# Normalising the input rows on ScalarE, moving four memory products between the first head products, and making the lower parts of the memory weights on VectorE

## The chip, the cores and the metric

The kernel runs on one core of one Trainium2 chip. The metric is device microseconds (us) of one execution, as the median of several runs; lower is better. In the profile PE is TensorE (products), PEld its weight loads, DVE is VectorE, ACT is ScalarE, POOL is GpSimd and SP is the engine that issues most DMAs.

## The reference

One inference step of a decoder layer (model width 1024) for 1024 prompt tokens and 8 decode tokens. Cut to what matters here:

```python
xp = layer_norm(x_prompt, ln_in_g, ln_in_b)          # 1024 rows of 1024
xs = layer_norm(x_sample, ln_in_g, ln_in_b)          # 8 rows
mk, mv = (mem @ w_kv)                                # 256 memory rows, w_kv 1024 x 2048: keys, values
proj = x @ w_in + b_in                               # q, k, v, o of 4 heads, 8 gates, pool input, x-attention q, branch gates
y_m = mLSTM(q, k, v, gates) ; y_p = pool_mix(u) ; y_x = attention(xq, mk, mv)
x = layer_norm(ALPHA * x + (g0*y_m + g1*y_p + g2*y_x) @ w_o)
x = layer_norm(ALPHA * x + conv_gated_ffn(x))
```

`layer_norm` takes a row's mean and variance, subtracts and divides, then applies a gain and an offset per feature. The memory's keys and values do not depend on x; they are needed by the outputs and by the attention, long after the mLSTM heads have begun.

## The kernel before, in words

**Units.** All large products are *units*: 128 output columns of some weight, times all token columns, in chunks of 384, 384 and 264 columns (CHUNKS, line 27). Each fp32 weight is split in two parts of 12 bits: an upper part `whi` (ScalarE, line 180) and a lower part `wlo` (line 181), and each k-tile takes three products (upper x upper, upper x x-lower, lower x upper), line 250. `s.pool` chooses the engine of the lower part: GpSimd or VectorE. A split is made in two pieces of 128x512. A memory unit (`kv_unit`, line 456) has one chunk of 256 columns, so 24 products; a head unit has 72; the gate unit has 48.

**The order.** `run_units` (line 183) writes all instructions out in one order, and every engine executes its own in that order. While it writes a unit's products it counts a planning clock, `max(n, 256) / 2400` us for each product of n columns, and after each 0.6 us or more of it calls `tick` (a piece of a weight split, up to NW = 3 weights ahead of the units done; then loads as far as buffers reach, 4 ahead for the memory weights, line 199) and then `side.advance`. Side work lies in two lanes of generators; each yields the planning time until its next step. Lane 0 is stepped before lane 1.

**The opening.** Units 0 to 15 are the memory units. `first` and `second` (lines 493, 499) load the first x tiles, later ones are loaded ahead of units 4 to 9 (line 507), the small rows at unit 10 (`load_rest`), and at unit 14 the gate weights are prepared on VectorE. The x rows lie in nine tiles of 128 tokens (tile 8: the 8 decode rows). Two generators run beside the units:

- `g_rows_in` (line 394, lane 0 from unit 1): step i takes the statistics of tile i on VectorE (`ln_stats`; the power -1/2 on GpSimd, line 366) and normalises tile i-1 in place on VectorE (`normalise`, line 370); then it yields 2.8.
- `g_ln_in` (line 409, lane 1 from unit 3): for each chunk of three tiles it waits until they are normalised, yields 2.0, and then `to_features` (line 377) for each of 8 feature blocks transposes on TensorE, applies gain and offset on ScalarE (`tmp`, line 384), rounds to `xhi` and subtracts to `xlo` on VectorE (lines 386, 387). It yields 1.0 after each block.

Behind the memory units comes the gate unit (line 621). Before each of its chunks it calls `wait_for`, which writes out side steps, without products between, until that chunk of x is there. `tmp` has 3 buffers, the small PSUM tiles 5, the products' PSUM tiles 3. After the gate unit the key and value rows are transposed (`g_kv_rows`, lane 1), and the units of the first head follow in the order k, k, v, v, q, q, o, o (line 783), then three more heads.

**Weights at the start.** The first two memory weights have their lower parts on VectorE, the other 14 on GpSimd (line 490).

Of the kernel before, what the change touches and what calls it, by code (L numbers as in the profile page):

```python
# [14 lines left out]
D = 1024  # L15
# [8 lines left out]
# Token columns, and their token tiles, of products whose rows a layer norm follows.  # L24
PASSES = (((640, 392), (8, 5, 6, 7)), ((256, 384), (2, 3, 4)), ((0, 256), (0, 1)))
# Token columns of one matrix product: three token tiles, three, two and the decode rows.
# [4 lines left out]
# Weights are loaded up to EARLY pieces ahead at the start; each piece is split in PARTS steps, not closer  # L31
# together than SHARE of a unit's length, nor sooner than AGE after its load.
EARLY = 4
PARTS = 2
SHARE = 0.1
AGE = 2.0
# Time, in us, between two looks at the side work.
# [3 lines left out]
class Side:  # L41
    """Work that is put between the large products: lanes of generators, each lane in order. A generator
    yields the time, in us of large products, that passes before its next step."""
# [45 lines left out]
class Split:  # L89
    """Weights, k-tiles of 128 rows and some columns, as two parts of 12 bits each, whose sum is the weight."""  # L90
# [16 lines left out]
def tile_hybrid_step(ctx: ExitStack, tc: tile.TileContext, x_prompt, mem_prompt, x_sample, cache_mem_k,  # L107
# [43 lines left out]
    # The tensor engine's clock rises after some microseconds of work: until the first loads are here.  # L151
# [9 lines left out]
    # ---------------------------------------------------------------- dense products  # L161
# [11 lines left out]
    def split_part(s, k):  # L173
        """One of the PARTS shares of the k-tiles."""
        if k == 0:
            s.hi = weight_tile(s, "whi", NW, F32R)
            s.lo = weight_tile(s, "wlo", NW, F32R)
        n = s.nk // PARTS
        ks = slice(k * n, (k + 1) * n)
        nc.scalar.activation(s.hi[:, ks], s.raw[:, ks], AF.Copy)  # L180
        (nc.gpsimd if s.pool else nc.vector).tensor_sub(s.lo[:, ks], s.raw[:, ks], raw_f(s.hi[:, ks]))  # L181

    def run_units(first_loads):
# [10 lines left out]
        def load_more(first=0):  # L194
            """Loads as far as the buffers reach."""
            while len(here) < len(order):
                n = len(here)
                s = order[n]
                if n < first or n < min(split + 2, free + NW + 1) or s.early and n < split + EARLY:
                    load(s)  # L200
                    here[n] = clock
                else:
                    break

        def tick(us, force=False):
            """Splits, a part at a time, as far as the buffers of the units before reach."""
            nonlocal split, part, clock, last
            clock += us
            if split not in here or not (split < free + NW or order[split].tile):
                return  # L210
            if not force and (clock - last < space or clock - here[split] < AGE):
                return
            last = clock
            split_part(order[split], part)
            part += 1
            if part == PARTS:
                split, part = split + 1, 0
                load_more()
# [55 lines left out]
    def weight_pairs(w2d, c0, ncols, k0=0, nk=8):  # L274
        """[(Split, column)] for each 128 columns of w2d[k0*128:, c0:c0+ncols]."""
        out = []
        wd = min(1024 // nk, ncols)
        for a in range(c0, c0 + ncols, wd):
            s = Split(w2d[k0 * 128:(k0 + nk) * 128, a:a + wd].rearrange("(k p) c -> p k c", p=128), nk, wd)
            out += [(s, c) for c in range(0, wd, 128)]  # L280
        return out
# [6 lines left out]
    # ---------------------------------------------------------------- vectors as columns  # L288
# [59 lines left out]
    # ---------------------------------------------------------------- layer norms  # L348
# [5 lines left out]
    def ln_stats(parts, n):  # L354
        """Mean and 1/deviation of the rows that parts hold side by side."""
        st = sp.tile([128, 2, 6], F32, name=nm("st"), tag="st")
        for i, p in enumerate(parts):
            nc.vector.bn_stats(st[:n, i, :], p)  # L358
        return mean_dev(st, len(parts), n)
# [17 lines left out]
    def to_features(rows, c0, n, g0, b0, wait, per=1):  # L377
        """Transposes normalised rows of one chunk, applies gain and offset, splits into xhi, xlo."""
        for f in range(8):
            p = PS()  # L380
            for j, (t, m) in enumerate(rows):
                nc.tensor.transpose(p[:, j * 128:j * 128 + m], t[:m, f * 128:(f + 1) * 128], ident[:m, :m])  # L382
            tmp = cur[0].tile([128, 392], F32, tag="tmp", bufs=3, name=nm("tmp"))
            nc.scalar.activation(tmp[:, :n], p[:, :n], AF.Identity, bias=colA[:, b0 + f:b0 + f + 1],
                                 scale=colA[:, g0 + f:g0 + f + 1])
            nc.vector.tensor_copy(xhi[:, f, c0:c0 + n], tmp[:, :n])  # L386
            nc.vector.tensor_sub(xlo[:, f, c0:c0 + n], tmp[:, :n], raw_f(xhi[:, f, c0:c0 + n]))  # L387
            if f % per == per - 1:
                yield wait * per
# [4 lines left out]
    def g_rows_in():  # L394
        """x, normalised, by token."""
        st = {}
        for i in range(10):
# [3 lines left out]
            if i:  # L401
                m = rows_of(i - 1)
                normalise(xt[i - 1][:m, :D], xt[i - 1][:m, :D], *st[i - 1], m)
# [3 lines left out]
    def g_ln_in():  # L407
        for c, (c0, n) in enumerate(CHUNKS):
# [3 lines left out]
            yield 2.0  # L412
# [9 lines left out]
    # ================================================================ phase 1: memory keys and values  # L422
# [43 lines left out]
    def g_kv_rows():  # L466
        """Keys and values by memory row, for the outputs and as the second factor of the attention."""
# [19 lines left out]

    for j, (s, c) in enumerate(weight_pairs(w_mem_kv[0], 0, 2048)):
        u = kv_unit(j, s, c)
        s.pool = j > 1  # L490
# [17 lines left out]
        if j == 10:  # L508
            u.before = load_rest
        if j == 14:  # L510
            u.before = lambda: (gate_prepare(), make_conv_cols())
        units.append(u)

    # ================================================================ phase 2: gates of the mLSTM
    # Per token of a tile: a, exp(-m), exp weight of the state, decay; by head. Tile 8: decode rows.
# [10 lines left out]
    class GateSplit:  # L526
        """Both parts of the gates' weights side by side, each multiplied with both parts of x."""
# [20 lines left out]
    def g_gates():  # L548
# [19 lines left out]
        # b: sum of lf within a tile of 128 tokens; mt: running max.  # L568
# [54 lines left out]
    units[-1].after = lambda: side.add(1, "kv_rows", g_kv_rows())  # L623

    # ================================================================ phase 3: mLSTM
# [30 lines left out]
    def halves(hi, lo, src, scale=None):  # L656
        """src, scaled by a column, as two parts of 12 bits each."""
# [7 lines left out]
    def product(out, w, x, first=True, last=True):  # L665
        """out (+)= w^T x, both in two parts."""
# [116 lines left out]
    for h in range(4):  # L783
        for wi, what in enumerate("kvqo"):
            off = {"q": 0, "k": 1024, "v": 2048, "o": 3072}[what] + 256 * h
            for kt, (s, c) in enumerate(weight_pairs(w_in2, off, 256)):
                units.append(head_unit(h, what, kt, s, c))
                if (h, wi, kt) == (0, 0, 0):
                    units[-1].before = lambda: next_phase("phase1")

    def g_sample_mlstm():
        """The decode rows: one step of the recurrence for each of the 32 states."""
# [37 lines left out]
        # For each decode row a block of 40 columns, zero but for the two parts of q: results 0-7 and 32-39.  # L830
# [91 lines left out]
    # ================================================================ phase 4: attention to the memory  # L922
# [91 lines left out]
    # Softmax of the decode rows, by memory row: for each a block of 16 columns with its two parts, else zero.  # L1014
# [109 lines left out]
    def open_gate(b, f):  # L1124
        """The spilled gates come back before their sigmoid."""
# [72 lines left out]
    # ================================================================ phase 5: mLSTM output  # L1198
# [34 lines left out]
    # ================================================================ phase 6: pooling  # L1233
# [5 lines left out]
    def pool_consts():  # L1239
        # sel[15 b + j, g, b'] = (b == b') and j >= 16 - window  # L1240
        nc.gpsimd.memset(sel, 1.0)
        for g in range(4):
            w = 2 << g
            v = sel[:, g, :]
            # 15 b + j - 15 b' - (16 - w) >= 0
            nc.gpsimd.affine_select(out=v, in_=v, pattern=[[-15, 8]], compare_op=OP.is_ge, fill=0.0,
                                    base=-(16 - w), channel_multiplier=1)
            # 15 b' + 14 - (15 b + j) >= 0
# [124 lines left out]
    # ================================================================ phase 7: w_o, first layer norm  # L1373
# [63 lines left out]
    # Each pass goes through the features in the other direction and starts with the weights that are still here.  # L1437
# [14 lines left out]
    # ================================================================ phase 8: gated feed-forward with convolution  # L1452
# [5 lines left out]
    def g_state_conv():  # L1458
        """The two kept rows of each decode row, feature-major: [feature, tile, row, decode row]."""
# [99 lines left out]
    # The first chunk's columns are normalised while the other two chunks are multiplied.  # L1559
# [30 lines left out]
    # ================================================================ phase 9: the last products by chunk, second layer norm  # L1590
# [9 lines left out]
    def ln2_half(t, h):  # L1600
        """Transposes features 512 h.. of a token tile and takes their share of its mean and deviation."""
# [91 lines left out]
```

## Time and profile before

| | |
|---|---|
| median of 3 runs | 2214.84 us (2213.61 to 2218.53) |
| span of the profiled execution | 2210.3 us, 36109 instructions |
| the profiled execution's own time | not listed apart; the three runs lie 3.3 to 8.2 us above the span |
| TensorE busy | 2169.0 us (98%) |
| VectorE, ScalarE, GpSimd busy | 55%, 37%, 16% |
| mean granted TensorE clock | 0.994 of full |

Span and busy times come from one execution under the profiler; the median comes from runs without it. A busy share is a mean over stages with different limits, so it says little of one stage. A wait is named by who waited and by what ended the wait.

### The profile page before, as it was taken

What the parts mean: (1) busy time and instruction counts of PE and PEld (TensorE: products, weight loads), DVE (VectorE), ACT (ScalarE), POOL (GpSimd) and SP (SyncE); (2) the same over time, 40 slices, a digit from 0 to 9 for tenths busy, and PEclk for the clock granted to TensorE, in tenths of its full rate; (3) what the DMA queues carried; (4) which work ended last, traced back from release to release, by engine and by line L of the source; (5) the groups of instructions that cost most, each with busy time, mean ns of one, the idle gap of its engine ahead of it and who ended that gap; (6) DMA issues with size and microseconds to landing.
All of it is one profiled execution on the core that took longest, in us unless ns stands there. A gap on an engine that the chain in (4) does not pass through costs nothing.

```text
span 2210.3 us, 36109 instructions
## 1 busy us (share of the span) xinstructions
PE 2169.0 (98%) x14337; PEld 2140.7 (97%) x14337; DVE 1207.6 (55%) x2776; ACT 826.1 (37%) x1635; POOL 364.5 (16%) x523
## 2 busy tenths in 40 slices
PE   8999999999999999999999999999999999999996
PEld 7899999999999999999999999999999999999996
DVE  6834738383767765635335556644544343443457
ACT  4524343434457543442213333444142341423421
POOL 6301010101110000211004734101010010101104
PEclk9999999999999999999999999999999999999998
DMA  9131232223367664649653223311111111111112
GB/s 264 55 106 53 58 72 53 63 61 70 90 187 260 193 193 159 217 173 339 189 165 103 87 77 86 87 49 49 42 45 49 49 49 48 39 52 45 49 49 77
DMA packets 267795, 229.50 MB, mean 104 GB/s; under 512 B 15669, under 2 KB 245863, under 8 KB 267611
## 3 DMA queue, kind: packets, MB, share of 16 engines
q1 hardware_dynamic: 261291, 208.12, 31.4%
q0 software_dynamic: 6336, 19.09, 2.3%
q8 instruction: 112, 1.84, 0.3%
q14 instruction: 56, 0.46, 0.1%
HBM read 177.13 MB, written 50.64 MB: 103 GB/s over the span
## 4 chain that ended last, share of the span: by engine, by line
PE 88%; DVE 4%; issue 3%; DMA 1%; SPq 1%; ACT 1%; POOL 1%; ACTq 0%; DVEq 0%; POOLq 0%
PE pd L250 79%; PE ps L668 1%; PE ps L669 1%; PE ps L670 1%; DMA Cs<-in_state_C_dram 1%; SPq L171 1%; DVE xlo L387 1%; PE ps L692 1%; PE ps L1086 1%; PE ps L878 1%; PE ps L382 0%; DVE st L358 0%; DVE xhi L386 0%; DVE wlo L181 0%; PE ps L688 0%
## 5 line engine op out<-in xcount | busy, mean ns | idle before, releaser
L250 PE MATMUL pd<-xhi,whi 128*128 128x384 f32 (+1 forms) x2784 | 897.3, 322 | 0.6 <-ACT gf L541 0.6
L250 PE MATMUL pd<-xlo,whi 128*128 128x384 f32 (+1 forms) x2784 | 895.0, 321 | 0.0
L250 PE MATMUL pd<-xhi,wlo 128*128 128x384 f32 (+1 forms) x2784 | 891.2, 320 | 0.0
L250 PEld LDWEIGHTS pd<-xhi,whi 128*128 128x128 f32 x2784 | 524.5, 188 | 1.9 <-ACT gf L541 0.8
L250 PEld LDWEIGHTS pd<-xlo,whi 128*128 128x128 f32 x2784 | 524.9, 189 | 0.1
L250 PEld LDWEIGHTS pd<-xhi,wlo 128*128 128x128 f32 x2784 | 524.3, 188 | 0.0
L181 DVE TENSOR_TENSOR wlo<-raw,whi 128x512 fp32r<-128x512 f32 (+1 forms) x326 | 227.0, 730 | 437.2 <-ACT whi L180 430.6
L180 ACT ACTIVATE whi<-raw 128x512 fp32r<-128x512 f32 (+1 forms) x382 | 219.4, 620 | 271.6 <-PE pd L250 201.4
L1490 ACT ACTIVATE hup<-pd 128x384 f32<-128x384 f32 (+1 forms) x132 | 60.4, 458 | 277.9 <-PE pd L250 277.7
L1503 DVE SCALAR_TENSOR_TENSOR cv<-hup,colB,cv 128x1023 f32<-128x1023 f32 x88 | 112.7, 1281 | 1.6
L1544 DVE TENSOR_TENSOR z<-pd,z 128x384 f32<-128x384 f32 (+3 forms) x120 | 59.5, 511 | 82.6 <-PE pd L250 82.6
L1500 POOL COPY tl<-hup 128x10 f32<-128x10 f32 x44 | 8.4, 192 | 519.6 <-ACT hup L1490 519.6
L366 POOL TENSOR_TENSOR rs<-rs,half 128x1 f32<-128x1 f32 (+2 forms) x60 | 38.0, 633 | 340.2 <-DVE rs L365 330.1
L1491 ACT ACTIVATE cv<-pd,colB 128x384 f32<-128x384 f32 (+1 forms) x132 | 83.6, 633 | 0.0
L181 POOL TENSOR_TENSOR wlo<-raw,whi 128x512 fp32r<-128x512 f32 x56 | 76.3, 1386 | 41.4 <-ACT whi L180 41.4
L1117 POOL DMA_DIRECT2D gD<-ch x60 | 32.8, 547 | 293.5 <-ACT ch L1116 274.4
L1509 POOL TENSOR_TENSOR cv<-cv,cv 128x1032 f32<-128x1032 f32 x22 | 53.1, 2414 | 112.6 <-DVE cv L1503 97.0
L250 PE MATMUL pd<-mh,whi 128*128 128x392 f32 (+2 forms) x192 | 62.7, 326 | 0.6 <-ACT mh L1338 0.6
L250 PE MATMUL pd<-ml,whi 128*128 128x392 f32 (+2 forms) x192 | 61.8, 322 | 0.1
L250 PE MATMUL pd<-mh,wlo 128*128 128x392 f32 (+2 forms) x192 | 61.5, 321 | 0.0
L1116 ACT ACTIVATE ch<-pd,colA 128x384 f32<-128x384 f32 (+1 forms) x60 | 32.7, 545 | 67.1 <-PE pd L250 56.2
L662 ACT ACTIVATE hh<-ps,colA 128x128 fp32r<-128x128 f32 x64 | 23.1, 360 | 79.7 <-DVE hh L663 75.0
(731 smaller groups left out, 4040.9 us busy)
## 6 DMA issues: line engine op xcount, KB each, us to landing
raw<-in_w_in_dram SPq DMA_DIRECT2D x72, 512.0 KB
raw<-in_w_up_dram SPq DMA_DIRECT2D x44, 512.0 KB
raw<-in_w_down_dram SPq DMA_DIRECT2D x22, 512.0 KB
raw<-in_w_o_dram SPq DMA_DIRECT2D x18, 512.0 KB
mx<-mixD SPq DMA_DIRECT2D x16, 516.0 KB
raw<-in_w_mem_kv_dram SPq DMA_DIRECT2D x16, 512.0 KB
Cs<-in_state_C_dram SPq DMA_DIRECT2D x32, 256.0 KB
out_dram<-Cs SPq DMA_DIRECT2D x32, 256.0 KB
```

Source lines behind the costliest of these rows:

```text
L180: nc.scalar.activation(s.hi[:, ks], s.raw[:, ks], AF.Copy)
L181: (nc.gpsimd if s.pool else nc.vector).tensor_sub(s.lo[:, ks], s.raw[:, ks], raw_f(s.hi[:, ks]))
L250: nc.tensor.matmul(p[:u.m, :n], lhsT=a, rhs=b, start=j == 0, stop=j == len(seq) - 1)
L366: nc.gpsimd.tensor_tensor(out=rs[:n], in0=rs[:n], in1=half[:n], op=OP.pow)
L662: nc.scalar.activation(hi, src, AF.Copy, scale=scale)
L1116: nc.scalar.activation(t[:, :n], p[:, :n], AF.Identity, bias=bias)
L1117: nc.gpsimd.dma_start(GD[b][f][:, c0:c0 + n], t[:, :n])
L1490: nc.scalar.activation(rw[:, c0:c0 + n], p[:, :n], AF.Copy)
L1491: nc.scalar.activation(cc[:, c0:c0 + n], p[:, :n], AF.Identity, bias=colB[:, 132 + ft:133 + ft], scale=colB[:, 88 + ft:89 + ft])
L1503: nc.vector.scalar_tensor_tensor(a, b[0], b[1], a, op0=OP.mult, op1=OP.add)
L1509: nc.gpsimd.tensor_mul(cc, CA.pop(j), cc)
L1544: nc.vector.tensor_add(Z2[f][:, cs], p[:, :n], Z2[f][:, cs])
```

## The change

Three things are changed, besides comments that are gone.

First, the x rows are normalised by one ScalarE instruction, (x times 1/deviation) plus (-mean/deviation). The second number, 128x1, is made by a small VectorE instruction (`minus_mean`, line 372), written out right after the next tile's statistics. `g_ln_in` yields 4.0 instead of 2.0 ahead of a chunk's transposes.

Second, only 12 memory units stand ahead of the gate unit. The other four follow the second k unit, the two v units and the first q unit of head 0, and the key and value rows are started after the last of them instead of after the gate unit. The small rows are loaded at unit 9 with the last x tile, and the gate weights are prepared at unit 11.

Third, the lower parts of all memory weights are made on VectorE.

```diff
+MEM_FIRST = 12
     def g_rows_in():
                 m = rows_of(i - 1)
-                normalise(xt[i - 1][:m, :D], xt[i - 1][:m, :D], *st[i - 1], m)
+                mv, rs = st.pop(i - 1)
+                nb = minus_mean(mv, rs, m)
+                nc.scalar.activation(xt[i - 1][:m, :D], xt[i - 1][:m, :D], AF.Identity, bias=nb[:m], scale=rs[:m])
                 ready.append(i - 1)
...
             while tiles[-1] not in ready:
                 yield 1.0
-            yield 2.0
+            yield 4.0
...
+    mem_late = []
     for j, (s, c) in enumerate(weight_pairs(w_mem_kv[0], 0, 2048)):
         u = kv_unit(j, s, c)
-        s.pool = j > 1
         s.early = True
...
-        if j == 10:
-            u.before = load_rest
-        if j == 14:
+        if j == 9:
+            u.before = lambda: (load_x(8), load_rest())
+        if j == MEM_FIRST - 1:
             u.before = lambda: (gate_prepare(), make_conv_cols())
-        units.append(u)
+        (units if j < MEM_FIRST else mem_late).append(u)
...
     units.append(Unit(GateSplit, 0, 8, mov_x, gate_evac, m=100,
                       need=lambda ci: wait_for(f"in{ci}")))
-    units[-1].after = lambda: side.add(1, "kv_rows", g_kv_rows())
...
                 units.append(head_unit(h, what, kt, s, c))
+                if mem_late and (wi, kt) != (0, 0):
+                    units.append(mem_late.pop(0))
+                    if not mem_late:
+                        units[-1].after = lambda: side.add(1, "kv_rows", g_kv_rows())
```

## Rows read from the trace of the kernel before

**Rows 1.** The page: busy time of each engine, its share of the span and its instructions.

```profile
PE 2169.0 (98%) x14337; PEld 2140.7 (97%) x14337; DVE 1207.6 (55%) x2776; ACT 826.1 (37%) x1635; POOL 364.5 (16%) x523
```

**Rows 2.** Busy time of each engine in four stretches: the length, then PE, PEld, DVE, ACT and POOL in us with their instruction counts, the granted TensorE clock as a share of full speed, the DMA share and GB/s.

```profile
30.00:81.60 51.60, 43.69 (x324) 41.16 (x324) 48.86 (x76) 26.82 (x52) 33.52 (x26) 0.93 0.40 117
81.60:90.00 8.40, 7.81 (x49) 7.24 (x50) 7.99 (x19) 4.72 (x10) 0.00 (x0) 1.00 0.64 182
90.03:175.00 84.97, 84.97 (x555) 84.52 (x556) 38.08 (x78) 24.03 (x37) 3.04 (x6) 1.00 0.32 95
32.50:36.00 3.50, 3.49 (x17) 3.49 (x18) 2.87 (x6) 1.34 (x2) 3.50 (x4) 0.51 1.10 335
```

**Rows 3.** The chain of work that ended last, from 0 to 130 us: start, length, what.

```profile
23.61 6.39 DMA x<-in_x_prompt_dram
30.02 1.30 DVE st L358 x2
...
31.74 0.73 DVE x L370
32.51 0.46 PE ps L382
...
45.18 1.53 DVE xlo L387
...
47.01 0.56 DVE xlo L387
...
61.94 3.27 DVE xlo L387
```

**Rows 4.** Groups of VectorE instructions by line and shape between 30 and 87.3 us: count, busy us, mean ns of one, idle time before them.

```profile
L387 DVE TENSOR_TENSOR xlo<-tmp,xhi 128x384 fp32r<-128x384 f32 x16 | 17.5, 1091 | 0.5
L386 DVE CAST xhi<-tmp 128x384 fp32r<-128x384 f32 x16 | 10.4, 651 | 0.6 <-ACT tmp L384 0.6
...
L370 DVE TENSOR_SCALAR x<-x,mv,rs 128x1024 f32<-128x1024 f32 x6 | 5.2, 871 | 0.2 <-issue 0.2
L387 DVE TENSOR_TENSOR xlo<-tmp,xhi 128x264 fp32r<-128x264 f32 x8 | 4.4, 555 | 0.3
L386 DVE CAST xhi<-tmp 128x264 fp32r<-128x264 f32 x8 | 4.0, 495 | 0.0
...
L370 DVE TENSOR_SCALAR x<-x,mv,rs 8x1024 f32<-8x1024 f32 x1 | 1.8, 1753 | 0.0
```

**Rows 5.** VectorE's instructions in order of time: start, length, line, operation, output<-inputs, count.

```profile
61.57 0.34 DVE L386 CAST xhi<-tmp 128x384 fp32r<-128x384 f32 x1
...
65.52 0.56 DVE L387 TENSOR_TENSOR xlo<-tmp,xhi 128x384 fp32r<-128x384 f32 x1
...
79.85 0.72 DVE L533 MEMSET gatew<- 128x800 f32 x1
...
81.50 1.28 DVE L181 TENSOR_TENSOR wlo<-raw,whi 128x512 fp32r<-128x512 f32 x2
...
86.93 0.43 DVE L387 TENSOR_TENSOR xlo<-tmp,xhi 128x264 fp32r<-128x264 f32 x1
...
88.74 0.55 DVE L544 TENSOR_TENSOR gi<-pd,gi 4x384 f32<-4x384 f32 x1 [0.17 <-ACT gf L541]
```

**Rows 6.** GpSimd's instructions in order of time, in the same form.

```profile
28.22 2.48 POOL L181 TENSOR_TENSOR wlo<-raw,whi 128x512 fp32r<-128x512 f32 x2
...
62.29 2.51 POOL L181 TENSOR_TENSOR wlo<-raw,whi 128x512 fp32r<-128x512 f32 x2
...
71.83 5.70 POOL L181 TENSOR_TENSOR wlo<-raw,whi 128x512 fp32r<-128x512 f32 x4 [1.81 <-ACT whi L180]
```

**Rows 7.** Groups of ScalarE instructions by line and shape over the whole span.

```profile
L180 ACT ACTIVATE whi<-raw 128x512 fp32r<-128x512 f32 x374 | 216.6, 624 | 271.6 <-PE pd L250 201.4 <-issue 41.0 <-DMA raw<-in_w_o_dram 14.0
...
L384 ACT ACTIVATE tmp<-ps,colA 128x384 f32<-128x384 f32 x32 | 21.1, 668 | 33.7 <-DVE xlo L387 18.3 <-PE ps L382 10.5 <-DVE z L1390 1.9
...
L1412 ACT ACTIVATE xn<-ps,nb,rs 128x512 f32<-128x512 f32 x16 | 11.5, 774 | 8.9 <-DVE nb L374 8.9
...
L1126 ACT ACTIVATE g0r<-g0r 128x1032 f32<-128x1032 f32 x8 | 8.5, 1064 | 27.9 <-DMA g0r<-gD 27.9
```

**Rows 8.** Line 374, the small product -mean/deviation where it already stands (the later layer norms): shortest, median and longest ns; then who waited for it, us in total and how often.

```profile
L374 DVE SCALAR_TENSOR_TENSOR nb<-mv,rs x18: 136/160/1209, 1350.9 to 2198.8; 128x1 f32<-128x1 f32 x16, 8x1 f32<-8x1 f32 x2
...
  ACT xn L1412: 26.8, 7
```

**Rows 9.** TensorE's instructions in order of time: the first product of the memory units 2 and 3 (two lines), the first gate product and the first head product.

```profile
17.45 0.28 PE L250 MATMUL pd<-memT0h,whi 128*128 128x256 f32 x1
...
20.33 0.36 PE L250 MATMUL pd<-memT0h,whi 128*128 128x256 f32 x1
...
81.64 0.42 PE L250 MATMUL pd<-xhi,gatew 128*100 128x384 f32 x1
...
90.03 0.41 PE L250 MATMUL pd<-xhi,whi 128*128 128x384 f32 x1 [0.62 <-ACT gf L541]
```

**Rows 10.** Who waited for whom from 0 to 130 us: us in total, times, longest; the last line is the DMA queue's own waits.

```profile
PE ps L382 <- DVE x L370: 6.7, 2, 4.3
DVE st L358 <- DMA x<-in_x_prompt_dram: 6.1, 3, 4.7
...
SPq L304 <- POOL wlo L181: 3.7, 2, 2.0
```

## The prediction

> **What bounds the kernel now.** The page comes first: TensorE is busy 98% of the span [rows 1], so only stretches in which it is not full can pay. The busy table by stretch shows where they lie: from 90.03 us on TensorE is busy all of 84.97 us, but from 30 to 81.6 us only 43.69 of 51.60 while VectorE has 48.86 of the 51.60 [rows 2]. Everything the change touches lies in this opening, before the first head product at 90.03 [rows 9]. Next the chain of waits: after x tile 3 has landed at 30.0 it runs through VectorE almost without a break (statistics, normalise, xhi, xlo) [rows 3]. There the same xlo of 128x384 takes 0.56, 1.53 or 3.27 us [rows 3]. Beside the longest, at 61.94, GpSimd makes two lower weight parts from 62.29 to 64.80 [rows 6]. So the opening is bound by VectorE, and VectorE loses time to GpSimd. Before 30 us it waits for the x tile's DMA [rows 3, 10]. The end I follow is the last xlo of the third chunk, 86.93 + 0.43 = 87.36 us [rows 5]; the gate product's last columns need it, and 2.7 us later the heads start.
>
> **What the change removes from VectorE, 30 to 87.36 us (57.4 us).** Unblocked durations are 0.56 (xlo) and 0.34 (cast) [rows 5], 0.43 (xlo of 264 columns) [rows 5] and, for casts of 264, no more than 0.34. Against them the groups hold 17.5 - 16 x 0.56 = 8.5, 10.4 - 16 x 0.34 = 5.0, 4.4 - 8 x 0.43 = 1.0 and 4.0 - 8 x 0.34 = 1.3 us too much [rows 4]: 15.8 us of blocking that goes if GpSimd makes no lower parts. The normalise goes too, 5.2 + 1.8 = 7.0 us [rows 4].
>
> **What it adds.** Lower parts: two of 128x512 take 1.28 us on VectorE [rows 5], where GpSimd needs 2.48 to 2.85 [rows 6]; for weights 7 to 11 and the twelfth, whose split falls in the gate unit, 6 x 1.28 = 7.7 us. The small product -mean/deviation, seven times: its row has 0.14 to 1.21, median 0.16 us [rows 8]. Here it is issued just behind the pair that starts GpSimd's power of the next tile, so I take 0.4, 2.8 us in all. On VectorE alone the sum is 57.4 - 15.8 - 7.0 + 7.7 + 2.8 = 45.1, a gain of 12.3 us.
>
> **The wait it adds.** ScalarE's normalise of tile i needs the small product, which stands on VectorE behind the statistics of tile i+1. ScalarE works in order: it has done all that was issued before, and stops there until VectorE arrives. VectorE then has nothing either: its next instruction is an xhi or a lower part, and both need a ScalarE result (tmp or upper part) that is queued behind the normalise. So at each tile VectorE stands for one normalise plus one tmp or upper part. No row has ScalarE on 128x1024 from SBUF with a bias and a scale: 1.06 is its 128x1032 sigmoid, 2 x 0.77 = 1.55 its two halves in the later layer norm [rows 7]. I take 1.06, nearest in form, and 0.57 for what follows (upper parts 0.62, tmp 0.67, less their overlap) [rows 7]: 1.63 us. Seven tiles, 2 to 8, are normalised after 30 us: 7 x 1.63 = 11.4 us. The row that shows such a stop: the later norms' ScalarE waited for the same small product 26.8 us in seven times [rows 8]. The bounds are 0 (ScalarE has other work) and 7 x (1.55 + 0.67) = 15.5 us.
>
> **The order at the end.** A memory unit counts 24 x 256 columns at 2400 per us, 2.56 us of the planner's time; twelve make 30.7. The norm steps come every 2.8 from 2.56, so tile 2 at about 11.5 and tile 8 at 28.2. Chunk 0's transposes start 4 later, at about 16, and end at 24; chunk 1's run from 28 past the end of the memory units into the gate unit; chunk 2's all come after the gates' second chunk, with no product left to cover them. Before, sixteen units made 41 us and covered them. So the sum is made again in the new order, from the start of tile 3's statistics at 30.02:
> - statistics to the start of the next normalise, 31.74 - 30.02 = 1.72 [rows 3], six tiles: 10.3
> - small product 2.8, waits 11.4
> - chunks 0 and 1: 16 features of 0.34 + 0.56 less 0.04 overlap: 13.8
> - lower parts of 7 to 11, two head weights and the twelfth: 8 x 1.2 (1.28 less overlap): 9.6
> - gate weights and the copy of the convolution columns: 81.50 - 79.85 = 1.65 [rows 5]
> - the gates' first two additions, 2 x 0.55 [rows 5]: 1.1
> - from the last xlo of chunk 1 to the first xhi of chunk 2: three ScalarE instructions (two gate evacuations, one tmp) of up to 0.67 [rows 7] and a transpose of 0.46 [rows 3], overlapped: 2.3
> - chunk 2: 8 x (0.43 + 0.29 less overlap) = 5.4
>
> Sum 58.3, so the third chunk is ready at 88.3 us, about where it was (87.36). The gates' first two chunks are by then done, and only the last products follow: heads at 88.7 instead of 90.03, a gain of 1.3 us.
>
> **The moved units.** Four memory units of 20.33 - 17.45 = 2.88 us [rows 9] leave a stretch in which TensorE had room and enter one in which it has none [rows 2]: 4 x 2.88 = 11.5 us on the path. Their weight splits there cost nothing: VectorE is busy 38.08 and ScalarE 24.03 of 84.97 us [rows 2]; without that cover each would cost 1.28. Their loads, and the key/value rows that start one after the other later (32 transposes either way), lie on queues with room, a DMA share of 0.32 [rows 2]. The eight small loads (convolution rows, gate weights and biases) move one unit ahead on SP's queue, to just behind x tile 8, and their use moves three units ahead. I cost that at nothing: VectorE comes to the gate weights only behind the statistics of all tiles. Were they late, VectorE would stand for no more than the one x tile's 6.39 us [rows 3].
>
> **Sum.** -1.3 + 11.5 = +10.2 us on the profiled execution, whose span is 2210.3 us. Its whole time is not listed apart; the three runs are 2213.6 to 2218.5, so 3.3 to 8.2 us lie around the span, and I add to the median: 2214.8 + 10.2 = 2225 us.
>
> **Rivals.**
> - Faster: ScalarE's stops cost VectorE nothing, because it still has work issued earlier. For it: VectorE saturated, ScalarE at 26.82 of 51.60 [rows 2]. Then 11.4 goes, 1.8 with it if the small product is 0.15, and x tiles whose load waited 3.7 us for GpSimd's release of a buffer [rows 10] land as much earlier: 10.2 - 16.9 = -6.7, 2208 us. It decides at 10.2 + 4.4 = 14.6 us off the opening. Against it: the issue order above. The Trainium skill (Perfetto Trace Analysis, Optimizing Scalar/DVE Operations) says that work may be worth offloading to ScalarE where DVE is saturated; it is saturated here, and by that rule this case would be the likely one.
> - About the same: half of the stops is hidden (-5.7) and the small product is short (-1.8): +2.7, 2217.5 us. For it: order within a step varies; the stop before the gate weights can be covered by them.
> - Worse: ScalarE's normalise is 1.55 (+3.4), the small product 1.21 (+5.7), and TensorE's clock is at its lower level as the heads begin, as after the stop of 4.3 us [rows 10], when it was 0.51 for 3.5 us [rows 2], costing 1.7: +21, 2236 us.
> - The change does not do what it says: the long xlo are not GpSimd's doing. Then 15.8 us stay: +26, 2241 us. Against it: where GpSimd rests, 82 to 90 us, the xlo is 0.43 and the pair 1.28 [rows 2, 5].
>
> The Trainium skill (SBUF — State Buffer, Who interferes with whom) says more against the change: a GpSimd instruction that reads SBUF fully blocks a VectorE instruction with two SBUF inputs. GpSimd keeps its powers, so by that rule a lower part or xlo can still be held at each tile. The small product's longest row, 1.21 [rows 8], fits; the sum above already has 0.4 for it, and by the rule it would be nearer 0.6, +1.4 us.
>
> **Chances and range.** Slower as computed 0.57, own range 2219.5 to 2231; about the same 0.21; faster 0.17; worse 0.03; not as said 0.02. What a measurement can tell from no change is 0.2%, 4.4 us, so 2210.4 to 2219.3 is the same. That gives slower 0.62, same 0.21, faster 0.17. The range 2209 to 2231 leaves out about half of the faster case and the two bad ones with the upper tail.
>
> **What would show it.** In the changed profile: xlo of 128x384 all near 0.56; GpSimd without lower parts; ScalarE's normalise waiting for the small product at every tile, some 1.5 us of VectorE idle behind each; the last xlo of chunk 2 near 88 us; first head product near 89; the four units at 2.9 us each between head products, TensorE without gaps from there. I am wrong if VectorE has no such gaps and the first head product comes before 78 us: then the four units are paid for.

## The result and the profile after

The changed kernel takes 2227.2 us (median, 2225.35 to 2228.07), the kernel before 2215.62 us (2213.61 to 2218.53) in the same comparison: a ratio of 1.0050, 95% interval 1.0038 to 1.0062. It is slower by 0.5%, some 11 us, with 2225 forecast and 2209 to 2231 as the range.

The busy table of the changed kernel, in the columns of [rows 2]:

```profile
30.00:81.60 51.60, 36.48 (x222) 33.37 (x222) 36.20 (x88) 29.48 (x49) 4.18 (x7) 0.87 0.35 105
81.60:90.40 8.80, 8.22 (x42) 5.20 (x41) 6.80 (x19) 5.49 (x10) 0.00 (x0) 1.00 0.00 0
91.00:175.00 84.00, 84.00 (x567) 83.86 (x567) 38.06 (x64) 28.49 (x46) 2.34 (x6) 1.00 0.27 70
```

VectorE was busy 48.86 of 51.60 us [rows 2] and is now busy 36.20. No engine is full between 30 and 81.6 us, and still the stretch is not shorter. That is what a chain of waits between two engines looks like. From 91 us on TensorE is full, as before.

The groups of VectorE up to 115 us, as in [rows 4]. In the file of the changed kernel L388 and L389 are the cast and the subtraction (L386 and L387 before), L376 is the small product and L407 ScalarE's normalise:

```profile
L389 DVE TENSOR_TENSOR xlo<-tmp,xhi 128x384 fp32r<-128x384 f32 x16 | 8.9, 558 | 0.6
L388 DVE CAST xhi<-tmp 128x384 fp32r<-128x384 f32 x16 | 5.7, 354 | 7.7 <-ACT tmp L386 7.7
...
L389 DVE TENSOR_TENSOR xlo<-tmp,xhi 128x264 fp32r<-128x264 f32 x8 | 3.5, 433 | 0.3
...
L376 DVE SCALAR_TENSOR_TENSOR nb<-mv,rs 128x1 f32<-128x1 f32 x8 | 1.2, 149 | 0.0
```

The xlo of 128x384 cost 17.5 us [rows 4] and cost 8.9 us now: the blocking is gone. In its place the casts stand 7.7 us for ScalarE's tmp. The waits between 30 and 90.5 us give the other half:

```profile
ACT x L407 <- DVE nb L376: 17.8, 7, 3.2
DVE wlo L183 <- ACT whi L182: 8.4, 4, 2.1
DVE xhi L388 <- ACT tmp L386: 7.7, 4, 2.1
```

ScalarE stands 17.8 us in seven times for the small product, and VectorE 8.4 + 7.7 = 16.1 us in eight times for ScalarE; the first of the eight is tile 1's stop, which ended at 29.41 us. One such round, first on VectorE and then on ScalarE, in order of time (in brackets: how long the engine stood before the instruction, and what ended that):

```profile
49.10 1.28 DVE L360 BATCH_NORM_STATS2 st<-x 128x6 f32<-128x512 f32 x2
50.41 0.21 DVE L365 BATCH_NORM_AGGREGATE mv<-st 128x2 f32<-128x12 f32 x1
50.66 0.15 DVE L367 TENSOR_SCALAR rs<-mv 128x1 f32<-128x1 f32 x1
50.73 0.15 DVE L376 SCALAR_TENSOR_TENSOR nb<-mv,rs 128x1 f32<-128x1 f32 x1
52.74 0.36 DVE L388 CAST xhi<-tmp 128x384 fp32r<-128x384 f32 x1 [1.86 <-ACT tmp L386]
```

```profile
50.91 1.24 ACT L407 ACTIVATE x<-x,nb,rs 128x1024 f32<-128x1024 f32 x1 [3.21 <-DVE nb L376]
52.06 0.65 ACT L386 ACTIVATE tmp<-ps,colA 128x384 f32<-128x384 f32 x1
```

While VectorE ends its last xhi and xlo and takes the statistics, ScalarE has nothing it may do (3.21 us). While ScalarE normalises and makes one tmp, VectorE has nothing it may do (1.86 us). The two engines take turns.

The end of the opening, again on VectorE:

```profile
81.61 0.56 DVE L389 TENSOR_TENSOR xlo<-tmp,xhi 128x384 fp32r<-128x384 f32 x1
83.87 0.55 DVE L548 TENSOR_TENSOR gi<-pd,gi 4x384 f32<-4x384 f32 x1 [1.71 <-ACT gf L545]
84.44 0.56 DVE L548 TENSOR_TENSOR gf<-pd,gf 4x384 f32<-4x384 f32 x1
84.92 0.28 DVE L388 CAST xhi<-tmp 128x264 fp32r<-128x264 f32 x1
...
89.97 0.43 DVE L389 TENSOR_TENSOR xlo<-tmp,xhi 128x264 fp32r<-128x264 f32 x1
```

All of chunk 2 lies behind the gates' second chunk, and the last xlo ends at 90.40 us (87.36 before, [rows 5]). The first head product, and the first and last product of one of the moved units, on TensorE:

```profile
90.65 0.34 PE L252 MATMUL pd<-xhi,whi 128*128 128x384 f32 x1
```

```profile
113.29 0.28 PE L252 MATMUL pd<-memT0h,whi 128*128 128x256 f32 x1
...
116.00 0.28 PE L252 MATMUL pd<-memT1h,wlo 128*128 128x256 f32 x1
```

So the heads start 0.62 us later than before [rows 9], and a moved unit takes 116.00 + 0.12 - 113.29 = 2.83 us among products that follow without a gap: 4 x 2.83 = 11.3 us. Together 11.9 us, against 11.1 us by the ratio (0.0050 x 2215).

### The profile page after: what moved, and what is told of

It reads as the page before. It is cut to its first block, busy times and chain, and to the rows that moved or that the text cites. A ratio compares the mean times of both kernels' runs of the same rounds, so it can differ in the third digit from the quotient of the medians.

```text
span 2224.8 us, 36127 instructions
## 1 busy us (share of the span) xinstructions
PE 2175.9 (98%) x14337; PEld 2144.5 (96%) x14337; DVE 1205.7 (54%) x2804; ACT 836.1 (38%) x1644; POOL 323.6 (15%) x495
## 4 chain that ended last, share of the span: by engine, by line
PE 90%; DVE 5%; DMA 2%; issue 1%; ACT 1%; POOL 1%; SPq 0%; ACTq 0%; POOLq 0%; DVEq 0%
PE pd L252 80%; PE ps L671 1%; PE ps L672 1%; PE ps L673 1%; DVE wlo L183 1%; DMA Cs<-in_state_C_dram 1%; PE ps L695 1%; PE ps L1093 1%; PE ps L885 1%; DVE xlo L389 0%; PE ps L384 0%; DVE st L360 0%; DVE xhi L388 0%; PE ps L691 0%; PE ps L697 0%
## 5 line engine op out<-in xcount | busy, mean ns | idle before, releaser
L183 DVE TENSOR_TENSOR wlo<-raw,whi 128x512 fp32r<-128x512 f32 (+1 forms) x354 | 245.2, 727 | 442.3 <-ACT whi L182 434.8
L183 POOL TENSOR_TENSOR wlo<-raw,whi 128x512 fp32r<-128x512 f32 x28 | 36.7, 1336 | 28.0 <-ACT whi L182 27.9
```

## The experiments

For every run below, the first head product in its trace, plus 11.3 us where four units follow behind it, less the 90.03 us of before [rows 9], is set against the measured ratio times 2215 us. If the opening is all that differs, the two agree.

| run | first head product, us | by the trace, us | ratio (95% interval) | by the ratio, us |
|---|---|---|---|---|
| the change | 90.65 | +11.9 | 1.0050 (1.0038 to 1.0062) | +11.1 |
| e1 normalise back on VectorE | 81.36 | +2.6 | 1.0019 (1.0010 to 1.0029) | +4.2 |
| e2 normalise ahead of the statistics | 79.53 | +0.8 | 1.0007 (0.9998 to 1.0016) | +1.6 |
| e3 sixteen units first | 96.27 | +6.2 | 1.0025 (1.0015 to 1.0035) | +5.5 |
| e4 lower parts back on GpSimd | 92.62 | +13.9 | 1.0062 (1.0047 to 1.0077) | +13.7 |
| e5 = e2 and e3 | 84.94 | -5.1 | 0.9977 (0.9969 to 0.9986) | -5.1 |
| e6 = e1 and e3 | 86.83 | -3.2 | 0.9983 (0.9974 to 0.9992) | -3.8 |
| e7 before, units moved alone | 83.68 | +5.0 | 1.0021 (1.0011 to 1.0031) | +4.7 |
| e8 before, normalise alone | 99.13 | +9.1 | 1.0033 (1.0021 to 1.0045) | +7.3 |
| e9 before, lower parts alone | 85.11 | -4.9 | 0.9966 (0.9952 to 0.9980) | -7.5 |
| e10 = e9 and e2's normalise | 84.83 | -5.2 | 0.9973 (0.9963 to 0.9984) | -6.0 |
| e11 = e10, x loaded earlier | 83.87 | -6.2 | 0.9972 (0.9962 to 0.9981) | -6.2 |

All twelve agree within their intervals, which reach some 2 to 3 us to either side. So what lies behind the first head product has to account for no more than that. Single traces leave as much: the profiled spans of the change and of before differ by 2224.8 - 2210.3 = 14.5 us, 2.6 more than 11.9.

**Theories.** A: the opening is bound by VectorE; ScalarE's normalise makes it stand at every tile, and the moved units cost their full length behind. B: the stops only fill time lost to loads or TensorE, and the loss is the moved units alone.

**e1: the normalise back on VectorE.**

```diff
-                mv, rs = st.pop(i - 1)
-                nb = minus_mean(mv, rs, m)
-                nc.scalar.activation(xt[i - 1][:m, :D], xt[i - 1][:m, :D], AF.Identity, bias=nb[:m], scale=rs[:m])
+                normalise(xt[i - 1][:m, :D], xt[i - 1][:m, :D], *st[i - 1], m)
```

> The changed kernel with the normalise back on VectorE, nothing else. Theory A (ScalarE's normalise makes VectorE stand at every tile, 2.0 to 2.2 us each): the seven stops of tiles 2 to 8 after 30 us go (-14), seven normalises of 0.72 us less the small product of 0.15 come (+4); the last xlo of chunk 2 moves from 90.4 to about 80 us and the time from 2227 to about 2217. Theory B (the stops only fill time that the opening loses anyway to loads or to TensorE, and the whole loss is the four moved units): the last xlo stays near 90 and the time at 2227.

The time is 2218.52 us, and the last xlo of chunk 2 moves to 80.67 + 0.43 = 81.1 us. VectorE does more work, and the heads start 9.3 us earlier. B falls.

**e2: the same instructions, the normalise ahead of the statistics.**

```diff
+            if i:
+                m = rows_of(i - 1)
+                mv, rs = st.pop(i - 1)
+                nb = minus_mean(mv, rs, m)
+                nc.scalar.activation(xt[i - 1][:m, :D], xt[i - 1][:m, :D], AF.Identity, bias=nb[:m], scale=rs[:m])
+                ready.append(i - 1)
             if i < 9:
                 m = rows_of(i)
                 st[i] = ln_stats([xt[i][:m, :512], xt[i][:m, 512:D]], m)
-            if i:
...
```

> The changed kernel with the two halves of a norm step exchanged: the small product and ScalarE's normalise of tile i-1 are written out ahead of the statistics of tile i. The same instructions run, only their order differs. Theory A (VectorE stands for a normalise plus a tmp because the statistics lie ahead of the small product): 1.7 us of statistics now cover each stop, so seven tiles give 7 x 1.7 = 12 us, the last xlo comes near 79 us and the time is about 2215, like the kernel before. Theory B (ScalarE's own work limits the opening, or loads do): no change beyond 2 us, 2225 to 2229.

2215.56 us. The same round in order of time on VectorE:

```profile
42.92 0.15 DVE L376 SCALAR_TENSOR_TENSOR nb<-mv,rs 128x1 f32<-128x1 f32 x1
42.99 1.28 DVE L360 BATCH_NORM_STATS2 st<-x 128x6 f32<-128x512 f32 x2
44.31 0.21 DVE L365 BATCH_NORM_AGGREGATE mv<-st 128x2 f32<-128x12 f32 x1
44.55 0.15 DVE L367 TENSOR_SCALAR rs<-mv 128x1 f32<-128x1 f32 x1
44.94 0.36 DVE L388 CAST xhi<-tmp 128x384 fp32r<-128x384 f32 x1 [0.24 <-ACT tmp L386]
```

The stop behind the small product is 0.24 us here instead of 1.86, and 0.24 to 0.51 at tiles 3 to 7, since the statistics now lie inside it. Behind the last small product, the decode rows', no statistics follow, and there VectorE still stands 1.86 us. The order alone is worth 11 us on the first head product. So it is not ScalarE's speed that costs, but what stands ahead of the small product on VectorE.

**e3: all sixteen memory units ahead of the gate unit** (the key and value rows follow the gate unit again).

```diff
-MEM_FIRST = 12
+MEM_FIRST = 16
...
-        if j == MEM_FIRST - 1:
+        if j == min(MEM_FIRST - 1, 14):
...
```

> The changed kernel with all sixteen memory units ahead of the gate unit, as before; lower parts on VectorE and the normalise on ScalarE stay. Theory A (the opening is bound by VectorE, TensorE has room there): the four units give back 11.5 us between the heads, cost VectorE four more weights in the opening (4 x 1.2 = +5) and cover the end of chunk 2 (-2): about 2219. Rival (TensorE has no room left in the opening): first head product 11 us later, 2227.

2220.45 us, and the first head product at 96.27: 5.6 us later, for 11.3 us that no longer follow. The rival, 11 us later, falls: TensorE had room for half of the units' time. The opening pays more than the 3 us that A had. What makes up the 5.6 us is not taken apart; four more weights' lower parts are 5 us of VectorE's time, and in this trace ScalarE also stood 4.45 us (up to 87.56) for the load of a head weight.

**e4: the lower parts back on GpSimd.**

```diff
         u = kv_unit(j, s, c)
+        s.pool = j > 1
         s.early = True
```

> The changed kernel with the lower parts of memory weights 2 to 15 back on GpSimd. Theory A1 (the blocking by GpSimd costs VectorE more than the lower parts do): xlo of 128x384 again at 1.5 us in most places, 8 to 16 us of blocking against 12 us of lower parts saved in the opening, 2223 to 2231. Rival A2 (the blocking falls into the stops that VectorE has anyway, so it costs nothing): the lower parts' 6 to 8 us after 30 us are won, about 2220.

2228.13 us. VectorE's groups from 30 to 92 us:

```profile
L389 DVE TENSOR_TENSOR xlo<-tmp,xhi 128x384 fp32r<-128x384 f32 x16 | 12.8, 799 | 0.5
L388 DVE CAST xhi<-tmp 128x384 fp32r<-128x384 f32 x16 | 7.9, 491 | 12.5 <-ACT tmp L386 12.5
...
L376 DVE SCALAR_TENSOR_TENSOR nb<-mv,rs 128x1 f32<-128x1 f32 x6 | 2.0, 337 | 0.0
```

The blocking returns, but with 12.8 us instead of the 17.5 of before [rows 4], since part of GpSimd's work falls into stops: its two pieces from 34.14 to 36.67 us lie in good part beside VectorE's stop from 35.44 to 38.62. The casts' wait for tmp grows from 7.7 to 12.5 us. A2 with its 2220 falls. A1 has the sign: the heads start 2.0 us later in the trace. But 0.0012 of the time lies within the intervals of the two ratios, and 1.23 us of the trace's difference can be the load of x tile 4, for which VectorE stood in e4 (up to 33.17) and not in the change.

**e5: e2 and e3 together.**

> The changed kernel with two things: the small product and ScalarE's normalise ahead of the next statistics (as in e2), and all sixteen memory units ahead of the gate unit (as in e3). Theory A (VectorE bounds the opening, the stops and the moved units are two separate losses, 11 and 6 us in e2 and e3): first head product near 85, against 96.3 in e3 less 11, with nothing of the memory left behind it: 2209 to 2211, faster than the kernel before by 4 to 6 us. Rival (with the stops gone TensorE bounds the opening when it has all sixteen units): first head product at 90 or later, 2214 or more.

2210.36 us, ratio 0.9977, and the first head product at 84.94. The two losses are separate and both can be taken back: 11.1 us in e2 and 11.3 - 5.6 = 5.7 us in e3 make 16.8 us, and by the trace e5 is 17.0 us better than the change. With both undone the rest of the change is a gain over the kernel before.

**e7, e8, e9: one part of the change alone, in the kernel before.** e7 has the unit list of the change; e8 the three lines that e1 takes out; e9 is one line:

```diff
-        s.pool = j > 1
```

> The kernel before with the four memory units alone moved between the first head products (with the loads and the gate weights one and three units earlier, as the change has them); lower parts on GpSimd, normalise on VectorE, 2.0 ahead of the transposes. Theory A: VectorE is freed of about 9 us of blocking by the four weights' lower parts, the end of chunk 2 loses its cover (+2), four units cost 11.5 behind: first head product near 82, about 2218. Rival (the moved units cost nothing, because their products fall into gaps): 2206.

> The kernel before with the normalise alone on ScalarE; sixteen units, lower parts on GpSimd, 2.0 ahead of the transposes. Theory A: stops of 2 us at seven tiles against seven normalises of 0.8 us saved, some of the blocking by GpSimd falling into the stops: first head product at 95 to 99, about 2221. Rival (ScalarE takes 7 us from a saturated VectorE at no price): first head product near 83, 2208.

> The kernel before with all lower parts of the memory weights on VectorE and nothing else. Theory A: 16 us of blocking go, nine weights' lower parts of 1.2 us (11) come after 30 us: first head product 4 to 5 us earlier, about 2210, faster than before. Rival (the lower parts cost VectorE as much as the blocking did): 2214 to 2216.

e7 takes 2220.55 us (expected 2218; the first head product at 83.7 instead of 82), e8 2223.18 (expected 2221, at 99.13), e9 2208.17 (expected 2210, at 85.1). All three have the sign of A, and the three rivals fall. By the ratios the parts alone add up to 0.0021 + 0.0033 - 0.0034 = 0.0020, not to 0.0050; by the first head products they add up to 5.0 + 9.1 - 4.9 = 9.2 of the 11.9 us. The 4.0 ahead of the transposes is in none of the three (e6 below bears on it). The normalise costs 9.1 us alone and 9.3 inside the change (90.65 less e1's 81.36), the units 5.0 and 5.7 (e3). The lower parts are worth 4.9 us alone and 2.0 inside (e4); the last xlo comes 7.7 us earlier by them alone and 1.3 inside. So in these traces freeing VectorE is worth little where VectorE stands for ScalarE. By the ratios (0.0034 and 0.0012) that difference is not clear of the intervals, and how much of the missing 2.7 us is the 4.0 was not tested.

**e6: of the change only the lower parts, the 4.0 and the earlier small loads are left.**

> The changed kernel with all sixteen memory units ahead of the gate unit and the normalise on VectorE: of the change only the lower parts on VectorE, the 4.0 ahead of the transposes and the earlier small loads are left. Theory A (the 4.0 pushes chunk 2 past the cover of the memory units, 1 to 3 us): 2209 to 2211, between e9 (2208) and the kernel before. Rival (the later transposes spare TensorE its stop at chunk 0 and pay for themselves): 2207 or less.

2210.33 us. Against e9 the last xlo of chunk 2 ends at 86.57 instead of 79.70 us, and the first head product is at 86.83 instead of 85.11. The time and the 1.7 us are as A said, and the rival's 2207 falls; the intervals of e6 and e9 overlap. That the 4.0 alone does it is not shown: the small loads come earlier too, and ScalarE stood 4.42 us in e6 (0.79 in e9) for the load of a head weight, with six of chunk 2's eight tmp written behind it.

**e10 and e11: is there more to gain?** e10 is e9 with e2's order and normalise; e11 has in addition:

```diff
-            u.before = lambda: (make_cols(), side.add(1, "ln_in", g_ln_in()))
-        if 4 <= j <= 9:
-            u.before = lambda i=j - 1: load_x(i)
+            u.before = lambda: (load_x(3), make_cols(), side.add(1, "ln_in", g_ln_in()))
+        if 4 <= j <= 8:
+            u.before = lambda i=j: load_x(i)
```

> The kernel before with all lower parts of the memory weights on VectorE (as e9), and the normalise on ScalarE with the small product and the normalise ahead of the next statistics (as e2); sixteen units, 2.0 ahead of the transposes. Theory A (VectorE bounds the opening; the statistics cover ScalarE's normalise): VectorE is spared nine times 0.72 less 0.15, about 5 us, less 0.2 to 0.5 us of stop at each tile; first head product 82 to 84 against 85.1, 2205 to 2207. Rival (TensorE bounds the opening once it has e9's pace): 2208, no difference from e9.

> e10 with x tiles 3 to 8 loaded one unit earlier, so ahead of one more memory weight in the DMA queue. Theory A (VectorE's and TensorE's stop before 30 us is x tile 3's arrival behind the weights): tile 3 lands about 1.6 us earlier (one weight of 512 KB at some 320 GB/s) and the first head product comes 1 to 2 us before that of e10. Rival (a memory weight then comes late instead): no difference from e10, TensorE waits for an upper part around 30 us.

e10 takes 2209.22 us, first head product at 84.83: a miss for A, and e9 is not beaten. The busy table of e9 and of e10 from 60 to 85 us:

```profile
60.00:85.00 25.00, 23.59 (x168) 21.55 (x169) 21.83 (x51) 16.85 (x33) 0.40 (x1) 1.00 0.32 86
```

```profile
60.00:85.00 25.00, 24.20 (x172) 21.95 (x171) 19.97 (x49) 17.81 (x34) 0.97 (x1) 1.00 0.34 92
```

VectorE has 1.9 us less to do in e10, and TensorE is busy 24.20 of 25 us. The last xlo ends at 79.43, 5.4 us ahead of the first head product: in this order TensorE sets the end by now. e11 takes 2208.30 us. In its trace the first head product comes 1.0 us before that of e10 and VectorE's stop of 3.35 us for x tile 3 is gone, as A said; by the times the two cannot be told apart. e9, one line, has the lowest ratio of all that was tried (0.9966), and e5, e6, e10 and e11 are not clear of it.

## Why the prediction was right, point by point

**What bounds the opening.** VectorE, blocked by GpSimd: shown. With the lower parts on VectorE the xlo of 128x384 take 0.558 us on average in the change, 0.56 forecast, and e9 alone brings the heads 4.9 us forward.

One reading of the kernel before was off: the end that the prediction followed there, the last xlo at 87.36 us, is not what the heads waited for. The busy table of before, in the columns of [rows 2]:

```profile
75.00:80.00 5.00, 5.00 (x38) 4.42 (x38) 4.78 (x8) 3.01 (x7) 3.44 (x3) 1.00 0.00 0
80.00:85.00 5.00, 5.00 (x34) 4.63 (x33) 4.83 (x14) 2.82 (x7) 0.00 (x0) 1.00 0.21 56
85.00:90.00 5.00, 4.41 (x31) 4.04 (x30) 4.66 (x12) 3.42 (x7) 0.00 (x0) 1.00 0.87 251
```

From 75 us on TensorE is full, but for the 0.62 us just ahead of the first head product, in which it waits for a gate evacuation on ScalarE [rows 9]. So TensorE and that evacuation end the opening there, and TensorE ends it in e9: its last xlo comes 7.7 us earlier than before, its heads only 4.9. In the changed kernel the end is where the prediction had it: the first head product follows the last xlo by 0.25 us.

**The wait it adds** was the step that decided, and it is as described. Only its size was off. The seven stops behind the small products of tiles 2 to 8 are 2.10, 2.10, 1.87, 1.86, 2.14, 2.10 and 1.86, 14.0 us instead of 11.4. Of the 2.6 us, 7 x 0.18 = 1.3 are the normalise, which took 1.24 us where 1.06 was forecast from a sigmoid. Some 1.0 more lie in the four stops of 2.1 us: in each, a memory unit's evacuation (0.36 us, kvT) stands on ScalarE between the normalise and the upper part or tmp, and the sum had no such term.

**The small product** was costed at 0.4 us a time and takes 0.15. Seven make 1.0 us instead of 2.8, which takes back 1.8 of the 2.6 us. The Trainium skill's rule (SBUF — State Buffer, Who interferes with whom) was read as lengthening it to 0.6; by that section the order of issue decides which of the two engines is held. In the change's trace the small product is not lengthened, and GpSimd's power starts only when it has ended. Where GpSimd also makes lower parts, in e4, the trace is in keeping with the rule: 0.56 and 0.86 us beside them, 0.15 us in the other four.

**The order at the end.** Chunk 2 uncovered behind the gates' second chunk: shown. From the last xlo of chunk 1 to the first xhi of chunk 2 it is 84.92 - 82.17 = 2.75 us, where 2.3 was forecast. The sum put the last xlo at 88.3 and the heads at 88.7; they came at 90.40 and 90.65. So the opening lost 0.6 us where a gain of 1.3 was forecast, because of the longer stops (2.6 us, less the 1.8 of the small product), the 0.45 us here and a start of tile 3's statistics at 30.62 instead of 30.02: tile 1's own stop had pushed it. These are 1.9 of the 2.1 us. That the time came within 2.2 us of the forecast is in part luck, as two terms were off in opposite directions. The small loads that move ahead cost nothing, as taken: VectorE stood 0.11 us ahead of the gate weights.

**The moved units.** 11.5 us forecast, 11.3 by the trace, and 5.7 us net of what they cost where they were (e3).

**The rivals.** The faster case would have had VectorE busy with earlier work during ScalarE's stops. It had none, and e2, where it has, is 0.0043 faster than the change. The rule that it cited (the Trainium skill, Perfetto Trace Analysis, Optimizing Scalar/DVE Operations) has the right condition, since VectorE was saturated (48.86 of 51.60 us), but the move paid nothing: e8 alone cost 0.0033. Even in the order that hides it, in e10, it gained nothing measurable on e9. The case of half-hidden stops did not come, since all seven are there in full. Nor did the worst: the normalise took 1.24 us, the small product 0.15, and the granted clock from 81.6 to 90.4 us was 1.00. The case that the long xlo are not GpSimd's doing is refuted by e9.

## What to carry to other kernels

When work moves from a full engine to an idle one, look at what each engine does between the hand-over and the hand-back: if the operand for the second engine is made behind other work on the first, both take turns and neither is full. Write the small operand out first, so that the first engine's own work covers the second's (11 us here for an exchange of two blocks). And before products are moved out of a stretch, ask where TensorE has room: here they left a stretch that had some for one that had none.

## What was not expected of the hardware

The lower parts on GpSimd held up VectorE for longer than the same work takes on VectorE itself. From 30 us on, e9 gives VectorE nine more weights' lower parts, 9 x 1.2 = 11 us, and its last xlo still ends 7.7 us earlier, with some 16 us of blocking gone. GpSimd's pieces are longer beside VectorE's work, too: a lower part of 128x512 took 1.24 us where VectorE waited for a load (two in 2.48 us at 28.22, [rows 6]) and 1.43 us in the four from 71.83 on, between VectorE's casts and subtractions. That VectorE holds up GpSimd there is the likely reason; no run tests it.
